# Strassen's seven block products for the output projections of both feed forwards

## The chip, the cores and the metric

One core of a Trainium2 chip runs the whole program. The metric is the device time of one execution in microseconds (us). Matmuls run on TensorE (PE), which writes to PSUM, a memory of 8 banks of 128 partitions x 512 fp32 here. VectorE (DVE), ScalarE (ACT) and GpSimd (POOL) do the elementwise work; DMAs are issued by SyncE (SP). The engines run their own queues in order and wait for each other by semaphores.

## The reference, cut to what matters

256 tokens of width 1024 pass through two transformer blocks. The last part of each block is a feed forward, and these two are what the change touches:

```python
def _swiglu(u, w_in, w_out):                       # first block, D_FF = 2816
    a = u @ w_in
    return (jax.nn.silu(a[..., :D_FF]) * a[..., D_FF:]) @ w_out

# second block, D_FF_2 = 4096
u = jnp.square(jax.nn.relu(jnp.einsum('bsd,df->bsf', h, w_mlp_in[l])))
x = x + gate_f * jnp.einsum('bsf,fd->bsd', u, w_mlp_out[l])
```

All values are fp32. In the first block the result is added to x without a gate.

## The kernel before

**Precision.** Every large matmul is made of three fp32r matmuls: an operand is split into a high part (a cast, `h` or `wh`) and a low part (the rest, `l` or `wl`), and `mm3` adds high x high, low x high and high x low into PSUM. `cols` loads weights by DMA into `raw` (128 x 1024), casts them on ACT to `wh` and subtracts on DVE to `wl`. So every 128 x 1024 piece of weights costs one DMA, one ACT step and one DVE step.

**A feed forward.** `ffn` walks over groups of hidden columns: 11 groups of 2 k-tiles (a k-tile is 128 hidden columns) in the first block, 8 groups of 4 in the second. The up projection (`dense_T`) makes the hidden values transposed: for a pair of k-tiles it takes 8 pieces of u, 2 columns of tiles and 3 matmuls each, 48 matmuls of 128x256 into one PSUM bank (twice that in the first block, which has two halves, the one through silu and the other one). Then come the elementwise steps: silu and a product in the first block (`glu`), relu and square in the second (`relu2`), and the split into `hT` high and low. The output projection (`out_steps`) takes one k-tile at a time: the hidden values of a k-tile are the stationary operand, 128 x 1024 of w_out the moving one, for both halves of the tokens. PSUM holds the 256 x 1024 result in 5 banks through the whole feed forward: two of 512 columns for the first 128 tokens, and 512, 256 and 256 for the second (`CUTS`). So a k-tile is 5 triples, 9 matmuls of 128x512 and 6 of 128x256. The last `lag` k-tiles finish the first half of the tokens ahead of the second, so that `resume` can start on it.

**What sets the order.** The code records operations, and a planner (`Plan.schedule`) puts them in order for each engine once, when the program is built, from its own costs and a table (`TUNING`, one row for each 140 of PE's large matmuls). `tt` records a tensor_tensor in two forms, and the planner takes DVE or POOL, whichever ends first by its costs. Buffers come from pools of slots: 37 of 4 KB a partition (`k4`), 14 of 2 KB, 12 of 1 KB, 8 PSUM banks. All operations are issued from one line, so the profile has a single line number, and groups are told apart by the tiles' names.

**The modulation** of the second block is computed in parts beside other work (`next_part`): four steps of 128x1024 on DVE a part (`raw<-raw,mod_c`). Six parts lie in the first feed forward and two in the second.

Of the kernel before, what the change touches and what calls it, by code (L numbers as in the profile page):

```python
# [40 lines left out]
def _constants():  # L41
# [63 lines left out]
FFN = [2] * 11  # L105
MLP = [4] * 8
# [167 lines left out]
class Plan:  # L274
# [362 lines left out]
class Net:  # L637
# [1012 lines left out]
    def swiglu(self, u, done):  # L1650
        nc, flow = self.nc, self.flow
        mods = []

        def swi(t, ac):
            sl = self.k(1, [P, S], nm="silu")
            nc.scalar.activation(sl, ac[:, :S], AF.Silu)
            yield
            nc.vector.tensor_tensor(sl, ac[:, S:], sl, ALU.mult)
            yield
            return sl  # L1660

        def glu(hT, aa, bb, n):
            sl = self.k(2, [P, n, S], nm="silu")
            nc.scalar.activation(sl, aa, AF.Silu)
            yield
            nc.vector.tensor_tensor(sl, bb, sl, ALU.mult)
            yield
            self.split(hT[0][0], hT[1][0], sl)
            yield

        def up(k0, n):
            hT = self.hidden(n)
            if k0 == 0:
# [11 lines left out]
        self.ffn("ffn", FFN, "w_ffn_out", up, done, LAG1, between)  # L1685


    def modulation(self):
# [78 lines left out]
    def block2_mix(self, x, u, done):  # L1767
# [263 lines left out]

        self.out_steps(self.out_accs(), [(act(k // 4), k, k) for k in range(KT)], "w_out_2", True, done, LAG2)

    def mlp(self, u, done):
        nc, flow = self.nc, self.flow

        def sq(t, ac):
            r, r2 = (self.k(2, [P, 512], nm="relu") for _ in range(2))
            nc.scalar.activation(r, ac, AF.Relu)
            yield  # L2040
            nc.vector.tensor_tensor(r2, r, r, ALU.mult)
            yield
            return r2

        def relu2(hT, i, ac):
            r, r2 = (self.k(2, [P, 2, S], nm="relu") for _ in range(2))
            nc.scalar.activation(r, ac, AF.Relu)
            yield
            nc.vector.tensor_tensor(r2, r, r, ALU.mult)
            yield  # L2050
            self.split(hT[0][0][:, 2 * i:2 * i + 2, :], hT[1][0][:, 2 * i:2 * i + 2, :], r2)
            yield

        def up(k0, n):
            hT = self.hidden(n)
            if k0 == 0:
                return hT, self.first_up(hT, u, n, [("w_mlp_in_2", 0)], sq)
            accs = self.dense_T(u, self.cols("w_mlp_in_2", k0 * P, (k0 + n) * P), n * P)
            return hT, [flow.start(relu2(hT, i, ac), "relu2") for i, ac in enumerate(accs)]

        def between(i):
            if 1 <= i <= 2:
                self.next_part()
            if i == 5:
                self.gate = self.mod(5)

        self.ffn("mlp", MLP, "w_mlp_out_2", up, done, 3, between)


LAG1, LAG2 = 6, 6  # L2070
MODF = (0, 2, 4, 5, 6, 7)
MODG = ((4, 0), (4, 1), (1, 0), (5, 0))

# [1 line left out]
def build(tc, a, out):  # L2075
    with ExitStack() as ctx:
        e = ctx.enter_context
# [7 lines left out]
        nc.lead = 0.0  # L2085
        n.setup()
        u, mem = n.mixer(x)
        u = n.memory_attention(x, u, mem)
# [78 lines left out]
```

## Time and profile before

| | us |
|---|---|
| median of 3 runs (762.37 to 763.64) | 762.38 |
| the profiled execution | 762.54 |
| its span | 760.7 |
| PE, DVE, ACT, POOL busy | 744.8, 571.7, 395.3, 42.0 |

The span runs from the first to the last instruction; the profiled execution's time has 1.8 us around it. Busy time of PE counts matmuls whose ends are modelled, and consecutive ones overlap, so the time of a matmul in a row is read from the start of one to the start of the next.

### The profile page before, as it was taken

To read this page: it belongs to the slowest core of one execution; us is meant where nothing else is said; L and a number is where in the kernel's file an instruction comes from. 1 tells how busy PE (TensorE), PEld (TensorE's weight loads), DVE (VectorE), ACT (ScalarE), POOL (GpSimd) and SP (SyncE) were. 2 spreads that over 40 slices of the span, in tenths; PEclk is the share of its full clock that TensorE was granted. 3 is DMA by queue.
4 is the path that set the end of the run, shared out by engine and by line. 5 is a ranking of instruction groups with operands and counts; after the bars stand their busy time and mean duration, and the time that the engine had idled before them with its cause. 6 is when DMAs were issued, how large, how long until landed. Compare 5 with 4: busy or idle time off the path is not lost.

```text
span 760.7 us, 13194 instructions
## 1 busy us (share of the span) xinstructions
PE 744.8 (98%) x5195; PEld 679.8 (89%) x5195; DVE 571.7 (75%) x936; ACT 395.3 (52%) x652; POOL 42.0 (6%) x50
## 2 busy tenths in 40 slices
PE   7999999999998999999999899999999999999998
PEld 5978899999897999999999788898887999999996
DVE  6999989799699995877453888887579976555512
ACT  6784774456387553443353646745347545454410
POOL 0012000000000000000000223021000000000000
PEclk9999999999999999999999999999999999999999
DMA  8828567965474887988868484555447777555401
GB/s 307 296 84 255 155 231 247 397 262 204 169 260 154 264 290 263 310 295 291 289 228 205 148 154 143 163 138 194 138 139 243 277 274 258 196 192 193 141 1 56
DMA packets 87763, 161.70 MB, mean 213 GB/s; under 512 B 8011, under 2 KB 44011, under 8 KB 87700
## 3 DMA queue, kind: packets, MB, share of 16 engines
q1 hardware_dynamic: 87700, 160.85, 64.6%
q8 instruction: 41, 0.67, 0.4%
q14 instruction: 22, 0.18, 0.1%
HBM read 159.75 MB, written 1.08 MB: 211 GB/s over the span
## 4 chain that ended last, share of the span: by engine, by line
PE 77%; DVE 11%; issue 6%; ACT 2%; DMA 2%; POOL 1%; SPq 0%; POOLq 0%; DVEq 0%; ACTq 0%
PE ps L634 77%; DVE wl L634 3%; DMA raw<-in_w_in_dram 2%; DVE s L634 1%; DVE sc L634 1%; DVE x L634 1%; DVE xn L634 1%; ACT wh L634 1%; DVE rp L634 1%; SPq L634 0%; POOL s L634 0%; DVE mk L634 0%; ACT prob L634 0%; DVE gt L634 0%; DVE aT L634 0%
## 5 line engine op out<-in xcount | busy, mean ns | idle before, releaser
L634 DVE TENSOR_TENSOR wl<-raw,wh 128x1024 fp32r<-128x1024 f32 (+4 forms) x237 | 279.1, 1203 | 66.0 <-ACT wh L634 49.5
L634 ACT ACTIVATE wh<-raw 128x1024 fp32r<-128x1024 f32 (+4 forms) x237 | 242.6, 1041 | 132.9 <-PE ps L634 30.3
L634 PE MATMUL ps<-aT,wh 128*128 128x256 f32 x1664 | 306.4, 284 | 0.0
L634 PEld LDWEIGHTS ps<-aT,wh 128*128 128x128 f32 x1664 | 257.9, 189 | 0.4 <-ACT wh L634 0.2
L634 PE MATMUL ps<-aT,wl 128*128 128x256 f32 x832 | 236.0, 284 | 0.0
L634 PE MATMUL ps<-wh,aT 128*128 128x512 f32 (+5 forms) x672 | 181.8, 357 | 2.1 <-ACT wh L634 1.3
L634 PEld LDWEIGHTS ps<-aT,wl 128*128 128x128 f32 x832 | 157.2, 189 | 0.5 <-issue 0.4
L634 PE MATMUL ps<-wh,hT 128*128 128x512 f32 (+1 forms) x540 | 140.1, 348 | 0.0
L634 PEld LDWEIGHTS ps<-wh,aT 128*128 128x128 f32 x672 | 118.6, 190 | 19.1 <-ACT wh L634 1.9
L634 PE MATMUL ps<-wl,aT 128*128 128x512 f32 (+5 forms) x336 | 117.3, 354 | 0.0
L634 PEld LDWEIGHTS ps<-wh,hT 128*128 128x128 f32 x540 | 93.9, 188 | 14.2
L634 PE MATMUL ps<-wl,hT 128*128 128x512 f32 (+1 forms) x270 | 94.1, 349 | 0.0
L634 PEld LDWEIGHTS ps<-wl,aT 128*128 128x128 f32 x336 | 63.5, 189 | 7.5
L634 DVE SCALAR_TENSOR_TENSOR raw<-raw,mod_c 128x1024 f32<-128x1024 f32 x48 | 57.3, 1218 | 6.8 <-DMA raw<-in_w_ada_dram 6.8
L634 PEld LDWEIGHTS ps<-wl,hT 128*128 128x128 f32 x270 | 50.7, 188 | 7.0
L634 POOL TENSOR_TENSOR s<-s,mhalf 128x1 f32<-128x1 f32 (+3 forms) x22 | 23.3, 1063 | 294.9 <-DVE s L634 284.2
L634 ACT ACTIVATE junk<-x 128x512 f32<-128x512 f32 (+1 forms) x29 | 16.1, 554 | 38.6 <-DVE x L634 36.5
L634 DVE TENSOR_TENSOR relu<-relu 128x512 f32<-128x512 f32 x16 | 10.9, 691 | 22.4 <-ACT relu L634 22.2
L634 ACT ACTIVATE prob<-ps,s 128x256 f32<-128x256 f32 (+1 forms) x48 | 20.0, 447 | 9.4 <-DVE s L634 9.4
L634 ACT ACTIVATE relu<-ps 128x512 f32<-128x512 f32 x16 | 9.5, 598 | 28.9 <-PE ps L634 28.3
L634 PE MATMUL ps<-ident,xn 128*128 128x128 f32 x96 | 19.4, 313 | 3.4 <-DVE xn L634 2.0
L634 ACT ACTIVATE hT<-silu 128x512 fp32r<-128x512 f32 x10 | 6.3, 632 | 31.0 <-DVE silu L634 31.0
(280 smaller groups left out, 647.1 us busy)
## 6 DMA issues: line engine op xcount, KB each, us to landing
raw<-in_w_in_dram SPq DMA_DIRECT2D x62, 512.0 KB, 6.3
raw<-in_w_ada_dram SPq DMA_DIRECT2D x48, 512.0 KB, 5.7
raw<-in_w_ffn_in_dram SPq DMA_DIRECT2D x44, 512.0 KB, 5.8
raw<-in_w_mlp_in_dram SPq DMA_DIRECT2D x32, 512.0 KB, 4.1
raw<-in_w_mlp_out_dram SPq DMA_DIRECT2D x32, 512.0 KB, 4.2
raw<-in_w_ffn_out_dram SPq DMA_DIRECT2D x22, 512.0 KB, 5.3
raw<-in_w_out_dram SPq DMA_DIRECT2D x16, 512.0 KB, 5.0
raw<-in_w_up_dram SPq DMA_DIRECT2D x6, 512.0 KB, 5.5
```

What stands on the lines that cost most here:

```text
L634: getattr(get[o.eng], name)(*map(real, args), **{k: real(v) for k, v in kw.items()})
```

## The change

For pairs of k-tiles the output projection becomes a product of 2 x 2 blocks. The hidden values are four blocks (two halves of the tokens, two k-tiles), the weights four (two k-tiles, left and right 512 columns), and the result four (two halves of the tokens, left and right columns). Strassen's scheme (in Winograd's form) needs seven block products in place of eight, from sums of blocks on both sides.

- `pair_sums` makes four more blocks of 128x128 from the four hidden blocks, then casts all that are needed (ACT) and takes the low parts (DVE: 128x384 and 128x512), in tiles `blocks`, `blockh`, `blockl`.
- `pair_weights` loads two rows of w_out as before and makes four sums of 128x512 (`sums<-raw,raw`, `raw<-raw`, `sums<-raw,raw`, `sums<-sums,raw`), each from two tensors in SBUF and by `tt`, so on DVE or POOL. Then it splits three pieces of 128x1024 and one of 128x512, where two of 128x1024 were split before.
- `pair_product` is 7 x 3 matmuls of 128x512. Each of the seven products has a PSUM bank of its own, in which all pairs add up; one bank is left for the up projections.
- `pair_end` forms the four result blocks from the seven banks and adds them to x, once for a feed forward.
- 9 of 11 pairs of the first feed forward and 14 of 16 of the second go this way; the last 2 pairs of each (`TAILF`, `TAIL`) go through `out_steps` as before, when the seven banks are free again.
- The order in the code is up projection p, then products of pair p - 2; in the first feed forward the first four products stand between the two up projections of a pair and three behind them.
- The planner's cost of a plain fp32 matmul has a floor of 0.213 in place of 0.109, one row of its table moves, and LAG1 is 4 in place of 6.

```diff
-            one = max(0.109, n / 600) if dt == F32 else max(0.054, n / 2250)
+            one = max(0.213, n / 600) if dt == F32 else max(0.054, n / 2250)
...
+    def pair_sums(self, a):
+        s = [a[:, i, :] for i in range(8)]
+        self.tt(s[4], s[0], s[2], ALU.add)
+        self.tt(s[5], s[1], s[0], ALU.subtract)
+        self.tt(s[6], s[4], s[1], ALU.subtract)
+        yield
+        self.tt(s[7], s[3], s[6], ALU.subtract)
+        yield
+        h, l = (self.k(4, [P, 8, P], F32R, nm=f"block{c}") for c in "hl")
+        for c in (slice(1, 4), slice(4, 8)):
+            self.nc.scalar.activation(h[:, c, :], a[:, c, :], AF.Copy)
+            self.nc.vector.tensor_tensor(l[:, c, :], a[:, c, :], h[:, c, :].bitcast(F32), ALU.subtract)
...
+    def pair_weights(self, w, k):
+        nc = self.nc
+        w0, w1 = (self.k(4, [P, DM], nm="raw") for _ in range(2))
+        for i, e in enumerate((w0, w1)):
+            nc.sync.dma_start(e, self.a[w][(k + i) * P:(k + i + 1) * P, :])
+        w2, w3 = self.k(4, [P, DM], nm="sums"), self.k(2, [P, 512], nm="sums")
+        lo, hi = slice(0, 512), slice(512, DM)
+        self.tt(w2[:, hi], w1[:, hi], w0[:, hi], ALU.subtract)
+        self.tt(w0[:, hi], w0[:, hi], w0[:, lo], ALU.subtract)
+        self.tt(w2[:, lo], w1[:, hi], w0[:, hi], ALU.subtract)
+        self.tt(w3, w2[:, lo], w1[:, lo], ALU.subtract)
+        out = []
+        for kb, e in ((4, w1), (4, w0), (4, w2), (2, w3)):
+            h, l = (self.k(kb, e.shape, F32R, nm=nm) for nm in ("wh", "wl"))
+            nc.scalar.activation(h, e, AF.Copy)
+            self.tt(l, e, h.bitcast(F32), ALU.subtract)
+            out.append((h, l))
...
+    BLOCKS = ((0, 1), (1, 3), (5, 6), (6, 5), (3, 2), (4, 4), (2, 7))
+    def pair_product(self, ps, blocks, w, first, last, which=slice(0, 7)):
+        for p, b in self.BLOCKS[which]:
+            self.mm3(ps[p], blocks[b], w[p], first, last)
...
+        for p in range(2, n):
+            self.main("mlp")
+            up(p)
+            if p - 2 < tail:
+                down(p - 2)
...
-LAG1, LAG2 = 6, 6
+LAG1, LAG2 = 4, 6
+TAIL, TAILF, LATE = 2, 2, 2
```

PE in the second feed forward. Before, the first 12 of a k-tile's 15 matmuls in the output projection (`ps` are the result's banks, `hT` the hidden values, `wh` and `wl` the weights):

```order
L634 MATMUL ps_7012<-wh_7380,hT_7496 128x512
L634 MATMUL ps_7012<-wh_7380,hT_7501 128x512
L634 MATMUL ps_7012<-wl_7393,hT_7496 128x512
L634 MATMUL ps_7020<-wh_7380,hT_7496 128x512
L634 MATMUL ps_7020<-wh_7380,hT_7501 128x512
L634 MATMUL ps_7020<-wl_7393,hT_7496 128x512
L634 MATMUL ps_7028<-wh_7380,hT_7496 128x512
L634 MATMUL ps_7028<-wh_7380,hT_7501 128x512
L634 MATMUL ps_7028<-wl_7393,hT_7496 128x512
L634 MATMUL ps_7035<-wh_7380,hT_7496 128x256
L634 MATMUL ps_7035<-wh_7380,hT_7501 128x256
L634 MATMUL ps_7035<-wl_7393,hT_7496 128x256
```

and now the first three of the seven products of a pair, behind the last matmul of an up projection:

```order
L634 MATMUL ps_8040<-aT_6866,wl_7938 128x256
L634 MATMUL ps_7106<-wh_7960,blockh_7894 128x512
L634 MATMUL ps_7106<-wh_7960,blockl_7902 128x512
L634 MATMUL ps_7106<-wl_7983,blockh_7894 128x512
L634 MATMUL ps_7114<-wh_7908,blockh_7894 128x512
L634 MATMUL ps_7114<-wh_7908,blockl_7902 128x512
L634 MATMUL ps_7114<-wl_7966,blockh_7894 128x512
L634 MATMUL ps_7121<-wh_7976,blockh_7894 128x512
L634 MATMUL ps_7121<-wh_7976,blockl_7902 128x512
L634 MATMUL ps_7121<-wl_7995,blockh_7894 128x512
```

A pair of k-tiles took 18 matmuls of 128x512 and 12 of 128x256; it now takes 21 of 128x512.

DVE in the second feed forward. Before, the steps for two pairs of k-tiles (four splits of the up projection's weights, four of the output's, in turns; square and split of the hidden values):

```order
L634 TENSOR_TENSOR wl_7517<-raw_7440,wh_7506 128x1024
L634 TENSOR_TENSOR wl_7540<-raw_7466,wh_7533 128x1024
L634 TENSOR_TENSOR wl_7561<-raw_7519,wh_7554 128x1024
L634 TENSOR_TENSOR wl_7590<-raw_7542,wh_7575 128x1024
L634 TENSOR_TENSOR wl_7608<-raw_7563,wh_7596 128x1024
L634 TENSOR_TENSOR wl_7629<-raw_7578,wh_7618 128x1024
L634 TENSOR_TENSOR wl_7657<-raw_7610,wh_7646 128x1024
L634 TENSOR_TENSOR wl_7684<-raw_7631,wh_7673 128x1024
L634 TENSOR_TENSOR relu_7707<-relu_7700 128x512
L634 TENSOR_TENSOR relu_7714<-relu_7709 128x512
L634 TENSOR_TENSOR hT_7721<-relu_7707,hT_7716 128x512
L634 TENSOR_TENSOR hT_7721<-relu_7714,hT_7716 128x512
```

and now the steps for one pair:

```order
L634 TENSOR_TENSOR wl_8044<-raw_7912,wh_7988 128x1024
L634 TENSOR_TENSOR wl_8058<-raw_7940,wh_8006 128x1024
L634 TENSOR_TENSOR sums_8046<-raw_7971,raw_7952 128x512
L634 TENSOR_TENSOR wl_8086<-raw_7971,wh_8029 128x1024
L634 TENSOR_TENSOR wl_8103<-raw_7952,wh_8080 128x1024
L634 TENSOR_TENSOR wl_8116<-sums_8046,wh_8096 128x1024
L634 TENSOR_TENSOR blocks_8129<-relu_8119 128x512
L634 TENSOR_TENSOR blocks_8129<-blocks_8129 128x128 x4
L634 TENSOR_TENSOR blockl_8144<-blocks_8129,blockh_8136 128x384
L634 TENSOR_TENSOR blockl_8144<-blocks_8129,blockh_8136 128x512
L634 TENSOR_TENSOR wl_8158<-sums_8089,wh_8123 128x512
```

A pair's steps on DVE went from six (four of 128x1024, two of 128x512) to 14.

POOL in the second feed forward, where it had no step before; now, for three pairs:

```order
L634 TENSOR_TENSOR sums_8046<-raw_7971,raw_7952 128x512
L634 TENSOR_TENSOR raw_7952<-raw_7952 128x512
L634 TENSOR_TENSOR sums_8089<-sums_8046,raw_7971 128x512
L634 TENSOR_TENSOR sums_8166<-raw_8091,raw_8074 128x512
L634 TENSOR_TENSOR raw_8074<-raw_8074 128x512
L634 TENSOR_TENSOR sums_8209<-sums_8166,raw_8091 128x512
L634 TENSOR_TENSOR blocks_8248<-blocks_8248 128x128
L634 TENSOR_TENSOR sums_8285<-raw_8211,raw_8196 128x512
L634 TENSOR_TENSOR raw_8196<-raw_8196 128x512
L634 TENSOR_TENSOR sums_8326<-sums_8285,raw_8211 128x512
```

Three of a pair's four sums of weights stand in POOL's queue, one in DVE's; DVE's one needs the first two of POOL's, and POOL's third needs DVE's.

## Rows read from the trace of the kernel before

**Rows 1.** The page: span, busy time by engine, the chain's shares.
```profile
span 760.7 us, 13194 instructions
PE 744.8 (98%) x5195; PEld 679.8 (89%) x5195; DVE 571.7 (75%) x936; ACT 395.3 (52%) x652; POOL 42.0 (6%) x50
...
PE 77%; DVE 11%; issue 6%; ACT 2%; DMA 2%; POOL 1%; SPq 0%; POOLq 0%; DVEq 0%; ACTq 0%
```

**Rows 2.** The chain in order of time: start, us, engine, tile, steps.
```profile
243.21 181.51 PE ps L634 x1345
...
575.68 179.29 PE ps L634 x1195
```

**Rows 3.** Busy time by stretch: stretch, length, then busy us and steps by engine.
```profile
core 0: us, PE busy (x) PEld busy (x) DVE busy (x) ACT busy (x) POOL busy (x), PEclk, DMA share, GB/s
242.00:428.60 186.60, 186.33 (x1388) 177.40 (x1388) 130.27 (x162) 83.74 (x105) 2.96 (x3) 1.00 0.79 253
...
576.00:757.00 181.00, 181.00 (x1213) 166.02 (x1211) 109.63 (x125) 77.94 (x93) 0.00 (x0) 1.00 0.54 182
```

**Rows 4.** Timeline of PE, one k-tile of an output product: start, us, step.
```profile
644.57 0.62 PE L634 MATMUL ps<-wh,hT 128*128 128x512 f32 x2
...
645.26 0.62 PE L634 MATMUL ps<-wh,hT 128*128 128x512 f32 x2
...
646.63 0.40 PE L634 MATMUL ps<-wh,hT 128*128 128x256 f32 x2
...
646.98 0.40 PE L634 MATMUL ps<-wh,hT 128*128 128x256 f32 x2
...
647.33 0.63 PE L634 MATMUL ps<-wh,hT 128*128 128x512 f32 x2
```

**Rows 5.** Timelines of DVE and POOL at 467.
```profile
466.94 3.49 DVE L634 TENSOR_TENSOR wl<-raw,wh 128x1024 fp32r<-128x1024 f32 x3
...
467.03 4.00 POOL L634 TENSOR_TENSOR rnat<-rp,rp 128x256 f32<-128x256 f32 x1 [4.46 <-DVE sp L634]
```

**Rows 6.** Timelines: 128x512 steps of DVE, and one of POOL.
```profile
753.51 1.28 DVE L634 TENSOR_TENSOR x<-x,gt 128x512 f32<-128x512 f32 x2
...
427.05 1.29 POOL L634 TENSOR_TENSOR xn<-x,modrow 128x512 f32<-128x512 f32 x1 [1.87 <-DVE x L634]
...
427.22 1.67 DVE L634 SCALAR_TENSOR_TENSOR xn<-xn,s,modrow 128x512 f32<-128x512 f32 x1
...
571.69 0.74 DVE L634 SCALAR_TENSOR_TENSOR xn<-xn,s,modrow 128x512 f32<-128x512 f32 x1
```

**Rows 7.** Groups by shape: busy us, mean ns, idle before; stretches 242:428, 600:740, 62:66.6.
```profile
L634 DVE SCALAR_TENSOR_TENSOR raw<-raw,mod_c 128x1024 f32<-128x1024 f32 x24 | 28.7, 1218 | 1.6 <-DMA raw<-in_w_ada_dram 1.6
...
L634 DVE TENSOR_TENSOR hT<-relu,hT 128x512 fp32r<-128x512 f32 x14 | 9.5, 692 | 0.3
L634 ACT ACTIVATE wh<-raw 128x1024 fp32r<-128x1024 f32 x46 | 47.9, 1056 | 46.5 <-DMA raw<-in_w_mlp_out_dram 21.1 <-DMA raw<-in_w_mlp_in_dram 16.1 <-PE ps L634 9.3
L634 ACT ACTIVATE relu<-ps 128x512 f32<-128x512 f32 x13 | 7.7, 597 | 25.7 <-PE ps L634 25.0
...
L634 DVE TENSOR_TENSOR wl<-raw,wh 128x536 fp32r<-128x536 f32 x1 | 1.3, 1260 | 0.0
```

**Rows 8.** Timeline of POOL, three places in the first 65 us.
```profile
23.48 0.46 POOL L634 TENSOR_TENSOR idxk<-rp,rp 128x128 f32<-128x128 f32 x1 [13.27 <-DVE rp L634]
...
49.23 2.83 POOL L634 TENSOR_TENSOR sp<-sp,ca 128x256 f32<-128x256 f32 x4 [20.40 <-DVE sp L634]
...
62.35 1.33 POOL L634 TENSOR_TENSOR qbn<-rp,rp 128x256 f32<-128x256 f32 x1 [3.20 <-DVE rp L634]
```

**Rows 9.** Timeline of DVE: the splits at the start of each feed forward.
```profile
243.74 1.21 DVE L634 TENSOR_TENSOR wl<-raw,wh 128x1024 fp32r<-128x1024 f32 x1
...
578.32 4.62 DVE L634 TENSOR_TENSOR wl<-raw,wh 128x1024 fp32r<-128x1024 f32 x4
```

**Rows 10.** Timeline of PE: the last output matmuls of each feed forward.
```profile
428.67 0.29 PE L634 MATMUL ps<-wl,hT 128*128 128x256 f32 x1
...
756.80 0.28 PE L634 MATMUL ps<-wl,hT 128*128 128x256 f32 x1
```

**Rows 11.** PE by stretch: length, busy us and steps, granted clock, DMA share, GB/s.
```profile
430.00:432.00 2.00, 1.24 (x3) 1.00 0.69 243
432.00:434.00 2.00, 0.97 (x4) 0.91 0.88 325
434.00:436.00 2.00, 2.00 (x9) 0.50 0.93 317
436.00:438.00 2.00, 2.00 (x8) 0.74 0.60 215
```

More of the change, by code (lines that the diff above doesn't have):

```diff
@@ new lines, in swiglu, with first, sums @@
+        tail = n - TAILF
+        blocks, pages, chains = {}, {}, {}
+        hT, ps = self.act_pair(), [self.acc() for _ in range(7)]
+        def first(t, ac):
+            o = yield from swi(t, ac)
+            pt, = yield from self.bank()
+            for j in range(2):
+                self.tr(pt[:, j * P:(j + 1) * P], o[:, j * P:(j + 1) * P])
+            self.pair_place(pages[0], pt[:, :S], t)
+            yield
+        def sums(p, *before):
+            yield from flow.after({0: list(before)})
+            blocks[p] = yield from self.pair_sums(pages[p])
@@ new lines, in silu, with glu @@
+        def silu(p, sl, ac):
+            nc.scalar.activation(sl, ac, AF.Silu)
+            yield
+        def glu(p, sl, ac):
+            yield from flow.after({0: chains["a", p]})
+            if p >= tail:
+                nc.vector.tensor_tensor(sl, ac, sl, ALU.mult)
+                yield
+                c, k = divmod(2 * (p - tail), 4)
+                self.split(*(e[c][:, k:k + 2, :] for e in hT), sl)
+                yield
+                return
+            pages[p] = self.pair_page()
+            flat = "p a b -> p (a b)"
+            nc.vector.tensor_tensor(pages[p][:, 0:4, :].rearrange(flat), ac.rearrange(flat), sl.rearrange(flat), ALU.mult)
+            yield
+            yield from sums(p)
@@ L1679, in between, with up, down @@
+        def up(p, part, fn, sl):
+            c0 = part * D_FF + p * S
+            ac, = self.dense_T(u, self.cols(w_in, c0, c0 + S), S)
+            chains["ab"[part], p] = flow.start(fn(p, sl, ac), "glu")
+        def down(p, which, w):
+            flow.need(chains["b", p])
+            self.pair_product(ps, blocks[p], w, p == 0, p == tail - 1, which)
         def between(i):
@@ L2034, in mlp, with squared @@
+    BLOCKS = ((0, 1), (1, 3), (5, 6), (6, 5), (3, 2), (4, 4), (2, 7))
+    def pair_product(self, ps, blocks, w, first, last, which=slice(0, 7)):
+        for p, b in self.BLOCKS[which]:
+            self.mm3(ps[p], blocks[b], w[p], first, last)
     def mlp(self, u, done):
         nc, flow = self.nc, self.flow
-        def sq(t, ac):
-            r, r2 = (self.k(2, [P, 512], nm="relu") for _ in range(2))
+        x, w_in, w_out = self.x, "w_mlp_in_2", "w_mlp_out_2"
+        n = 2 * sum(MLP) // 4
+        tail = n - TAIL
+        blocks, pages, hT = {}, {}, self.hidden(4)
+        def squared(ac, out):
+            r = self.k(2, [P, 512], nm="relu")
@@ L2039, in sq @@
             nc.scalar.activation(r, ac, AF.Relu)
             yield
[L2041 removed]
+            nc.vector.tensor_tensor(out, r, r, ALU.mult)
             yield
[L2043 to L2047, printed above, removed]
[L2048 to L2052 removed]
@@ L2054, in up, with first @@
[L2054 to L2062, printed above, removed]
+        def first(t, ac):
+            o = self.k(2, [P, 512], nm="relu")
+            yield from squared(ac, o)
+            pt, = yield from self.bank()
+            for j in range(4):
+                self.tr(pt[:, j * P:(j + 1) * P], o[:, j * P:(j + 1) * P])
+            for p in range(2):
+                self.pair_place(pages[p], pt[:, p * S:(p + 1) * S], t)
+            yield
@@ new lines, in sums, with pair, plain @@
+        def sums(p, *before):
+            yield from flow.after({0: list(before)})
+            blocks[p] = yield from self.pair_sums(pages[p])
+        def pair(p, ac):
+            pages[p] = self.pair_page()
+            yield from squared(ac, pages[p][:, 0:4, :].rearrange("p a b -> p (a b)"))
+            yield from sums(p)
+        def plain(p, ac):
+            o = self.k(2, [P, 2, S], nm="relu")
+            yield from squared(ac, o)
+            at = slice(2 * (p - tail), 2 * (p - tail) + 2)
+            self.split(hT[0][0][:, at, :], hT[1][0][:, at, :], o)
+            yield
@@ new lines, in mlp, with up, down @@
+        chains = {}
+        def up(p):
+            ac, = self.dense_T(u, self.cols(w_in, 2 * p * P, (2 * p + 2) * P), 2 * P)
+            chains[p] = flow.start((pair if p < tail else plain)(p, ac), "relu2")
+        ps = [self.acc() for _ in range(7)]
+        def down(p):
+            w = self.pair_weights(w_out, 2 * p)
+            flow.need(chains[p])
+            self.pair_product(ps, blocks.pop(p), w, p == 0, p == tail - 1)
+        self.main("mlp")
+        pages.update({p: self.pair_page() for p in range(2)})
@@ new lines, in mlp @@
+        wf = self.held(w_in, 0, 4 * P)
+        firsts = []
+        for t in range(NT):
+            flow.need(self.norms[t])
+            ac = self.acc()
+            self.dense_t(u, t, wf, ac)
+            firsts.append(flow.start(first(t, ac), f"first_{t}"))
+        for p in range(2):
+            chains[p] = flow.start(sums(p, *firsts), "relu2")
+        for p in range(2, n):
+            self.main("mlp")
+            up(p)
+            if p - 2 < tail:
+                down(p - 2)
+            if p in (4, 6):
@@ new lines, in pair_end, with add @@
+    def pair_end(self, ps, x, g=None):
+        nc = self.nc
+        tt = nc.vector.tensor_tensor
+        k = lambda: self.k(2, [P, 512], nm="sum")
+        p1, p2, p3, p4, p5, p6, p7 = ps
+        lo, hi = slice(0, 512), slice(512, DM)
+        def add(c, t, s):
+            if g is not None:
+                self.tt(c, c, g[:, s], ALU.mult)
+            self.tt(x[:, t, s], x[:, t, s], c, ALU.add)
+        c1, u = k(), k()
+        nc.scalar.activation(u, p1, AF.Copy)
+        tt(c1, p2, u, ALU.add)
+        tt(u, p6, u, ALU.add)
+        yield
+        u3 = k()
+        tt(u3, p7, u, ALU.add)
+        c4, c3 = k(), k()
+        nc.scalar.activation(c4, p5, AF.Copy)
+        tt(u, p5, u, ALU.add)
+        yield
+        tt(c3, u3, p4, ALU.subtract)
+        self.tt(c4, c4, u3, ALU.add)
+        tt(u, p3, u, ALU.add)
+        yield
+        add(c3, 0, lo)
+        add(c4, 0, hi)
+        add(c1, 1, lo)
+        add(u, 1, hi)
+        yield
```

66 lines of the change are left out of this document (50 added, 16 removed).

## Prediction

> **What bounds the kernel now.** I read the page first: TensorE (PE) is busy 98% of the span, VectorE (DVE) 75%, and the chain of waits lies on PE for 77% [rows 1]. The chain in order of time then says where PE alone sets the end: two stretches of some 180 us, which are the two feed forwards [rows 2]. The windows give these stretches a size: 186.6 us for the first, in which PE is never idle and DVE is busy 130 us, and 181.0 us for the second, with DVE busy 110 us [rows 3]. So what PE loses there is time won, as long as DVE, which feeds it, does not become the slower one: it has 56 and 71 us to spare. GpSimd (POOL) does 3.0 us of work in the first and none in the second. The profiled execution took 762.54 us (span 760.7); the median of the runs shown is 762.38. My sum is made against 762.54, and 0.2 us between the two decides nothing.
>
> **What PE saves.** A triple of 128x512 matmuls takes 0.69 us from start to start (644.57 to 645.26), a triple of 128x256 0.35 (646.63 to 646.98) [rows 4]. A k-tile of an output product has 3 triples of the first kind and 2 of the second: 2.77 us; from 644.57 to 647.33 it is 2.76. Two k-tiles cost 5.53 us. Seven block products cost 7 x 0.69 = 4.83. The gain is 0.70 us a pair. There are 9 pairs in the first feed forward and 14 in the second, so 23 x 0.70 = 16.1 us. The up projections keep their matmuls. If nothing else held PE, the time would be 762.5 - 16.1 = 746.4.
>
> **What DVE and POOL are given.** Steps of DVE in a row: three of 128x1024 take 3.49 us [rows 5], that is 1.14 apart; two of 128x512 take 1.28 [rows 6], 0.60 apart. By the line through these two, 128x384 takes 0.47 and 128x128 0.20. A step of the modulation with its accumulator read takes 28.7/24 = 1.20 [rows 7].
>
> Second feed forward, counted in the order of the changed kernel, from the first split of its weights to the last split that a block product needs. DVE: 70 of 128x1024 (79.8), 8 of the modulation (9.6), 49 of 128x512 (29.4), 14 of 128x384 (6.6), 40 of 128x128 (8.0), together 133 us. POOL: 49 of 128x512 and 16 of 128x128. A steady pair is 9.3 us of DVE (five 1024, four 512, one 384, three or four 128) beside 5.7 + 4.8 = 10.5 us of PE (16 triples of 0.35 for the up projection, then the products). DVE alone would just keep up. ScalarE has five casts of 1.06 us, a relu of 0.60 and two casts of blocks, some 7 us, and is no bound [rows 7].
>
> The question is whether POOL's steps run beside DVE's. Nearly all of both read two tensors in SBUF, and the trace has such meetings. POOL starts a 128x256 addition at 467.03, just behind the start of three weight splits on DVE, and ends at 471.03, 0.6 us after the last of them: 4.00 us instead of 0.71 [rows 5, 8]. At 427.22 DVE starts a 128x512 step while POOL is in one that takes 1.29; DVE's takes 1.67, where the same form takes 0.74 at 571.69 [rows 6]. And a 128x536 split takes 1.26 us where the 512-wide ones take 0.69, beside a POOL step begun at 62.35 [rows 7, 8]. Against that, four POOL steps at 49.23 ran at 0.71 each [rows 8] while DVE mostly read PSUM or a single tensor. I read it so: two such steps exclude each other, and the times add up.
>
> **The price of a POOL step.** Between the ends lies what it costs DVE: 0.93 us (1.67 - 0.74) and its whole 1.29 for 128x512. I take 1.20: in the first meeting POOL was already 0.17 us into its step when DVE started, which makes 1.10, and a handover from POOL to DVE or back will not be free. For 128x128, between nothing and the 0.46 of a step at 23.48 [rows 8]; I take 0.38. The second feed forward then has 49 x 1.20 + 16 x 0.38 = 64.9 us of POOL to put between 133 us of DVE: 198 us. A steady pair is 9.3 + 3 x 1.20 = 12.9 us and a little for blocks, against 10.5 of PE.
>
> The Trainium skill (SBUF — State Buffer, section Who interferes with whom) says that a VectorE instruction with two SBUF inputs and a GpSimd instruction that reads SBUF exclude each other, and that whoever comes first keeps the shared port for the whole instruction. By that rule the price is the whole 1.29 and 0.46, and the sum below would be 6 us higher for the second feed forward and 3 for the first. The trace agrees on the exclusion, but its one blocked DVE step lost 0.93.
>
> **The sum.** Before, DVE takes up this work at 578.32 [rows 9]. Nothing ahead of the feed forward is made shorter, so 578.3 + 198 = 776.5 is when the last split is there. PE then still has three of the seven products (2.1; the step that the last split feeds is fifth in the order) and four ordinary k-tiles (11.1): 789.7. From PE's last matmul to the end of the span it was 760.7 - 756.8 = 3.9 [rows 10]: 793.6, **33 us later** than now. The sums at the end (15 steps of DVE, 9 us) are hidden by the 11.1 us of the four k-tiles; without that cover some 4 us of them would show.
>
> First feed forward, counted the same way. DVE: 63 of 128x1024 (71.8), 24 of the modulation (28.8), 36 of 128x512 (21.6), 9 of 128x384 (4.2), 27 of 128x128 (5.4), two of 256 (0.7): 132 us. POOL: 26 of 128x512 (31.2), two of 128x1024 (2.4 each, twice a 512), 9 of 128x128 (3.4): 39 us. DVE starts at 243.74 [rows 9], so the last split is there at 415; behind it PE has half of an up projection (8 triples, 2.8), three products (2.1) and four k-tiles (11.1): 431. The matmuls of the present one end at 429.0 [rows 10]. That is +2. DVE's queue also has the product of the two up projections, which frees the one PSUM bank: it waits for the last 8 triples of PE (2.8 us) behind the last weight split, with one step of 1.2 us between. That is up to 1.6 us idle in each of 9 pairs, 0 to 14; POOL can use part of it, and I take 5. So **+7 us**.
>
> The remaining edits (a planner's cost for plain fp32 matmuls, one window of its table moved, the lag at the end) reorder steps in stages where PE is not short of work; I put them at 0, +-2. DMA carries the same weights. 762.5 + 33 + 7 = **802.5 us**.
>
> **The rivals.**
> (a) *POOL runs beside DVE.* Then a pair is bound by PE and the time is 746, or 750 with some waits at the ends. It decides at the point where DVE and POOL together fit into PE's pair: (10.5 - 9.3) / 3 = 0.4 us for a 128x512 step of POOL. For it speaks that the four steps at 49.23 were not hindered; against it the three meetings, each with more than 0.4 lost [rows 5 to 8]. Chance 0.13.
> (b) *The exclusion holds, but costs the low end:* 49 x 0.93 and nothing for the small ones is 46 us, 19 less than in the sum; the first feed forward then is bound by PE about as now. 802.5 - 19 - 7 = 776. It needs handovers without loss and no wait of DVE for PE. Chance 0.15.
> (c) *The single PSUM bank adds to the forecast:* DVE, late with its queue, frees the bank late, PE's next up projection waits, and DVE then waits for that. The full 14 us in the first feed forward and 1 us a pair in the second: 802.5 + 9 + 14 = 825. PE's clock can add to it: at 430 to 434 PE was busy 2.2 of 4 us, and the granted clock then stood at 0.50 (1.2 of 2.4 GHz) for two us and at a mean of 0.74 for two more [rows 11]. In a steady pair PE would be idle 2.4 us, so such a fall costs only where it is longer than the spare time. Chance 0.08.
> (d) That the change does not do what it says I leave out: the order shows 483 matmuls on blocks, 23 x 21.
>
> **How the numbers follow.** The forecast, DVE and POOL taking turns, has 0.64; its own range is 787 (price 0.93, no idle bank waits in the first feed forward) to 818 (price 1.29, 14 us of bank waits). For 8 in 10 I add (b) and most of (c): 770 to 825, with (a) and the far end of (c) left out. A measurement of this kernel tells 0.2% (1.5 us) from no change. Faster is (a): 0.13. Within 0.2% is a corner between (a) and (b): 0.02. Slower is the rest: 0.85.
>
> **What would show it.** Right: in the second feed forward DVE and POOL are busy nearly all the time, DVE's 128x512 and 128x1024 steps have means well above 0.69 and 1.22 us or POOL's stand far above 1.29, PE waits for DVE's wl in every pair and a pair lasts about 13 us; the first feed forward loses less than the second. The block products take 4.83 us a pair wherever PE does not wait. Wrong: PE still busy all through both stretches, with steps of DVE at 0.69 and 1.22 while POOL works; then (a). If PE's long waits are for the bank's release (silu or blocks) and not for wl, it is (c).

## The result, and the profile after

The changed kernel takes **829.88 us** (median; 828.0 to 831.79), 1.088 times the time of before (95% interval 1.0853 to 1.0908). The prediction was 802.5, with a range of 770 to 825: the direction was right, the size 27 us short, and the time lies 5 us outside the range. The profiled execution took 831.79 us, of which the span is 830.0.

The page of the changed kernel, the lines that answer to [rows 1]:

```profile
span 830.0 us, 13258 instructions
PE 759.3 (91%) x4988; PEld 681.6 (82%) x4988; DVE 740.2 (89%) x1112; ACT 443.0 (53%) x730; POOL 210.4 (25%) x152
...
DVE 22%; PE 16%; issue 4%; POOL 3%; ACT 2%; DMA 1%; POOLq 0%; SPq 0%; DVEq 0%; ACTq 0%
```

The chain of this profile is followed back only to 418 us, so its shares cover about half of the span; in that half DVE has more of it (22%) than PE (16%), where PE had 77% of the whole before, and POOL has 3%. DVE is busy 168 us longer and POOL 168. The busy time by stretch says where; the stretches are the first feed forward, the stage between, and the second (columns as in [rows 3]):

```profile
240.00:452.00 212.00, 193.17 (x1319) 179.35 (x1318) 191.20 (x235) 105.54 (x136) 62.60 (x42) 0.94 0.69 230
452.00:609.00 157.00, 148.81 (x845) 125.92 (x844) 128.61 (x219) 82.30 (x154) 26.76 (x19) 0.97 0.56 146
609.00:830.00 221.00, 185.88 (x1078) 164.71 (x1076) 211.01 (x224) 105.74 (x138) 105.63 (x63) 0.92 0.45 150
```

In the second feed forward DVE is busy 211 of 221 us and POOL 106, where it was 108 and nothing before. The granted clock of PE, 1.00 in both stretches of [rows 3], is now 0.94 and 0.92. The edges give the losses. The first feed forward's last output matmul starts at 451.91 and not 428.67 [rows 10]: +23.2. DVE's first split for the second feed forward starts at 608.90 and not 578.32 [rows 9]: +30.6, so the stage between gave 7.3. From there to the end it was 182.4 us and is 221.1: **+38.7**. (The expectations below say 22.6 and 8 for the first two; they took the edge a little earlier.)

What the second feed forward is made of stands in its groups of DVE and POOL by shape (busy us, mean ns):

```profile
L634 DVE TENSOR_TENSOR wl<-raw,wh 128x1024 fp32r<-128x1024 f32 x60 | 96.2, 1633 | 0.0
L634 DVE TENSOR_TENSOR wl<-sums,wh 128x1024 fp32r<-128x1024 f32 x14 | 24.1, 1724 | 0.0
L634 DVE TENSOR_TENSOR blockl<-blocks,blockh 128x512 fp32r<-128x512 f32 x14 | 18.1, 1296 | 1.1 <-ACT blockh L634 1.0
...
L634 POOL TENSOR_TENSOR sums<-sums,raw 128x512 f32<-128x512 f32 x14 | 30.6, 2189 | 48.4 <-DVE sums L634 48.2
L634 POOL TENSOR_TENSOR sums<-raw,raw 128x512 f32<-128x512 f32 x15 | 29.8, 1987 | 1.6 <-DVE wl L634 1.2 <-DMA raw<-in_w_mlp_in_dram 0.3
L634 POOL TENSOR_TENSOR raw<-raw 128x512 f32<-128x512 f32 x14 | 25.9, 1849 | 1.6 <-DVE sums L634 0.6
```

A split that took 1.22 us takes 1.63, and POOL's steps stand at 1.85 to 2.19, where one that was under way before DVE's next step took 1.26 (at 240.06). That is what the prediction asked for as a sign of turns being taken. The other sign, PE waiting for wl in each pair, is not there: PE's long waits name blocks in the first feed forward and relu in the second (us in total, times, longest). The last sections come back to that.

```profile
PE ps L634 <- DVE blocks L634: 12.7, 6, 4.7
...
PE ps L634 <- ACT relu L634: 22.6, 9, 6.1
```

### The profile page after: what moved, and what is told of

Same layout as the page of the kernel before. It is cut to its first block, busy times and chain, and to the rows that moved or that the text cites. A ratio compares the mean times of both kernels' runs of the same rounds, so it can differ in the third digit from the quotient of the medians.

```text
span 830.0 us, 13258 instructions
## 1 busy us (share of the span) xinstructions
PE 759.3 (91%) x4988; PEld 681.6 (82%) x4988; DVE 740.2 (89%) x1112; ACT 443.0 (53%) x730; POOL 210.4 (25%) x152
## 5 line engine op out<-in xcount | busy, mean ns | idle before, releaser
L634 PE MATMUL ps<-aT,wh 128*128 128x256 f32 x1664 | 327.5, 296 | 39.0 <-ACT relu L634 22.6
L634 DVE TENSOR_TENSOR wl<-raw,wh 128x1024 fp32r<-128x1024 f32 (+4 forms) x235 | 308.8, 1344 | 12.4 <-ACT wh L634 10.3
L634 ACT ACTIVATE wh<-raw 128x1024 fp32r<-128x1024 f32 (+4 forms) x237 | 242.0, 1037 | 102.7 <-POOL raw L634 28.7
L634 PE MATMUL ps<-wl,blockh 128*128 128x512 f32 x161 | 63.4, 394 | 1.0 <-DVE wl L634 1.0
L634 PE MATMUL ps<-wh,blockl 128*128 128x512 f32 x161 | 63.5, 394 | 0.0
L634 PE MATMUL ps<-wh,blockh 128*128 128x512 f32 x161 | 63.4, 394 | 0.0
L634 ACT ACTIVATE blockh<-blocks 128x384 fp32r<-128x384 f32 (+1 forms) x46 | 26.6, 578 | 68.7 <-DVE blocks L634 59.7
L634 POOL TENSOR_TENSOR sums<-sums,raw 128x512 f32<-128x512 f32 x21 | 46.3, 2204 | 54.0 <-DVE sums L634 53.8
L634 ACT ACTIVATE wh<-sums 128x1024 fp32r<-128x1024 f32 (+1 forms) x46 | 38.8, 842 | 34.3 <-DVE sums L634 18.7
L634 DVE TENSOR_TENSOR wl<-sums,wh 128x1024 fp32r<-128x1024 f32 (+1 forms) x31 | 49.3, 1599 | 0.0
L634 POOL TENSOR_TENSOR raw<-raw 128x512 f32<-128x512 f32 x21 | 39.4, 1878 | 20.2 <-DVE sums L634 19.2
L634 POOL TENSOR_TENSOR blocks<-blocks 128x128 f32<-128x128 f32 x25 | 17.7, 712 | 94.4 <-DVE blocks L634 60.7
L634 DVE TENSOR_TENSOR blockl<-blocks,blockh 128x384 fp32r<-128x384 f32 (+1 forms) x46 | 38.4, 836 | 2.2 <-ACT blockh L634 1.9
```

The source lines that it names most:

```text
L634: getattr(get[o.eng], name)(*map(real, args), **{k: real(v) for k, v in kw.items()})
```

## The experiments

### All pair steps on DVE, and each feed forward alone

```diff
 # dve_only: in pair_sums, pair_weights and pair_end
-        self.tt(w2[:, hi], w1[:, hi], w0[:, hi], ALU.subtract)
+        self.nc.vector.tensor_tensor(w2[:, hi], w1[:, hi], w0[:, hi], ALU.subtract)
...
 # mlp_only: swiglu as before; ff1_only: mlp as before
```

> The change with all sums and splits of the pairs on DVE, none on POOL. If DVE and POOL take turns (a POOL step of 128x512 costs about 1.20 us of DVE's time, the same step on DVE 0.60), the second feed forward gets 49 x 0.60 + 16 x 0.18 = 32 us shorter and the first up to 26 x 0.60 + 2 x 1.26 + 9 x 0.18 = 20: about 778 us, between 765 and 795. If POOL's steps run beside DVE's and the loss has another cause (the one PSUM bank), DVE has 75 x 0.60 + 25 x 0.20 = 50 us more to do and the time is 830 or more.

Measured **770.65 us** (ratio 1.0101, 1.0085 to 1.0117): 59 us less than the change, with 1213 steps on DVE in place of 1112. So POOL's help was the greater part of the loss; 8 us of it stay without that help. The same groups of DVE in the second feed forward, now alone in their stage:

```profile
L634 DVE TENSOR_TENSOR wl<-raw,wh 128x1024 fp32r<-128x1024 f32 x60 | 71.5, 1210 | 0.0
...
L634 DVE TENSOR_TENSOR wl<-sums,wh 128x1024 fp32r<-128x1024 f32 x14 | 16.9, 1210 | 0.0
...
L634 DVE TENSOR_TENSOR blockl<-blocks,blockh 128x512 fp32r<-128x512 f32 x14 | 9.5, 678 | 0.2
```

These three groups alone are 40.5 us shorter, with the same steps. And the two feed forwards by stretch:

```profile
243.00:424.00 181.00, 180.20 (x1302) 169.03 (x1300) 178.00 (x265) 104.54 (x135) 2.04 (x2) 1.00 0.83 269
576.00:749.00 173.00, 165.90 (x1030) 145.05 (x1028) 172.57 (x266) 104.27 (x138) 0.00 (x0) 0.99 0.54 186
```

In the first, PE is busy 180.2 of 181 us, and most of the 9 x 0.70 = 6.3 us that PE was to save are there: its last output matmul starts at 423.01 and not at 428.67 [rows 10], 5.7 us earlier. (DVE's last step that reads the output banks starts at 423.38, where it was 429.93, 6.6 earlier.) In the second DVE is busy 172.6 of 173 us and is the bound by itself: from its first split there (576.26) to the end (767.0) are 190.7 us, 8 more than the 182.4 of before.

> Block products in the second feed forward alone, the first as before. The trace of the changed kernel puts 38.7 us of the loss behind the start of the second feed forward's splits, 22.6 ahead of the end of the first and 8 between: about 803 us. By the prediction on record (33 and 7 us) 795.5. If the two stages disturb each other (the planner's order is made anew for the whole program), it is neither.

> Block products in the first feed forward alone, the second as before. By the trace of the changed kernel 762.4 + 22.6 + about 6 of the stage behind it = 791 us; by the prediction on record 769.5.

Measured **804.45** (1.0549, 1.0534 to 1.0565) and **787.69** (1.0328, 1.0311 to 1.0345). The two losses, 41.8 and 25.1 us, add up to 66.9 of the 67.5 of the change. So the stages hardly disturb each other, and the first feed forward's part is 23 to 25 us, more than three times what the prediction gave it.

### POOL steps that nothing waits for

```diff
 # pool_adds: dve_only, and in pair_weights of the second feed forward
+            more = self.k(2, [P, 512], nm="more")
+            for _ in range(3):
+                nc.gpsimd.tensor_tensor(more, w1[:, lo], w1[:, hi], ALU.add)
 # pool_memsets: eight of these instead
+                nc.gpsimd.memset(more, 0.0)
 # pool_copies: three of these instead
+                nc.gpsimd.tensor_copy(more, w1[:, hi])
```

> The kernel with all pair steps on DVE, and in each of the 14 pairs of the second feed forward three additions of 128x512 on POOL that nothing uses (both operands from the loaded weights in SBUF). DVE has no idle time in that stage. If a POOL step keeps DVE out, 42 x 1.07 us (the price read from the changed kernel's trace: 52.5 us of longer DVE steps for 49 POOL steps) = 45 us come on top of 770.6: 816, between 42 x 0.93 and 42 x 1.29 = 810 to 825. If POOL runs beside DVE, 771, at most 774.

> The same with eight memsets of 128x512 on POOL in each pair in place of the three additions: POOL is busy as long (112 x 0.48 = 54 us), but reads no tensor. If it is the reading of two tensors in SBUF that excludes, 771 to 774. If any POOL step, or the order and the semaphores around it, costs DVE time, 810 or more.

> The kernel with all pair steps on DVE, and in each pair of the second feed forward three copies of 128x512 on POOL from SBUF to SBUF, that nothing uses: one tensor read where the additions read two and the memsets none. If any read of SBUF by POOL keeps DVE out, 42 steps cost some 42 x 0.7 to 1.3 us: 800 to 825. If it takes two operands on POOL's side too, 769 to 774.

Measured **813.08** with additions (1.0664, 1.065 to 1.0679), **769.93** with memsets (1.0097, 1.0081 to 1.0112), **786.49** with copies (1.0318, 1.0303 to 1.0334). Against dve_only an addition costs 42.4 / 42 = 1.01 us, a copy 15.8 / 42 = 0.38, and 112 memsets nothing. The copies fit neither of their two forecasts (800 to 825, 769 to 774). No engine uses the results, and nearly all of the cost is the meeting itself: with the additions DVE is busy 37.9 us longer (740.8 for 702.9). In two places, 5.1 us together, DVE waits for a buffer that a POOL step still holds. The timeline of DVE in the kernel with additions shows it step by step; POOL's row is first:

```profile
654.76 28.23 POOL L634 TENSOR_TENSOR more<-raw 128x512 f32<-128x512 f32 x6 [3.36 <-DMA raw<-in_w_mlp_out_dram]
...
668.33 1.21 DVE L634 TENSOR_TENSOR wl<-raw,wh 128x1024 fp32r<-128x1024 f32 x1
669.46 0.67 DVE L634 TENSOR_TENSOR wl<-sums,wh 128x512 fp32r<-128x512 f32 x1
670.07 1.21 DVE L634 SCALAR_TENSOR_TENSOR raw<-raw,mod_c 128x1024 f32<-128x1024 f32 x1
671.21 0.07 DVE L634 DVE_READ_ACCUMULATOR raw<-raw,mod_c 128x1 f32 x1
671.21 2.30 DVE L634 SCALAR_TENSOR_TENSOR raw<-raw,mod_c 128x1024 f32<-128x1024 f32 x1
...
673.44 2.27 DVE L634 SCALAR_TENSOR_TENSOR raw<-raw,mod_c 128x1024 f32<-128x1024 f32 x1
...
675.64 2.27 DVE L634 SCALAR_TENSOR_TENSOR raw<-raw,mod_c 128x1024 f32<-128x1024 f32 x1
...
677.85 1.74 DVE L634 TENSOR_TENSOR sums<-raw,raw 128x512 f32<-128x512 f32 x1
679.51 1.22 DVE L634 SCALAR_TENSOR_TENSOR mod_s<-mod_s,mod_b 128x8 f32<-128x8 f32 x1
680.65 1.21 DVE L634 TENSOR_TENSOR wl<-raw,wh 128x1024 fp32r<-128x1024 f32 x1
681.78 1.76 DVE L634 TENSOR_TENSOR raw<-raw 128x512 f32<-128x512 f32 x1
...
729.13 1.73 DVE L634 TENSOR_TENSOR wl<-sums,wh 128x512 fp32r<-128x512 f32 x1 [3.86 <-POOL more L634]
```

POOL has six steps in 28.23 us, and six steps of DVE are longer by 1.06 to 1.09 us than the same forms elsewhere (2.30 for 1.21; 1.74 and 1.76 for 0.67; 1.22 for a step of 128x8 that took 0.15 in dve_only). One POOL step is one lengthened DVE step, whatever the DVE step's size.

The Trainium skill (SBUF — State Buffer, section Who interferes with whom) limits the exclusion to a GpSimd instruction that reads SBUF, which is how the memsets came to be the test. By that rule they cost nothing, and the trace agrees. By the same rule an addition or a copy should lock DVE out for its whole length. Here both fall 0.2 us short of it. While DVE stands still, an addition takes 1.26 us and a copy 0.62; where they meet a DVE step, they lengthen it by 1.06 to 1.09 and by 0.40. So the copy is cheaper because it is shorter. The rows of pool_copies, a copy alone and a DVE step that met one (1.62 for 1.21):

```profile
710.57 0.62 POOL L634 COPY more<-raw 128x512 f32<-128x512 f32 x1
...
629.31 1.62 DVE L634 SCALAR_TENSOR_TENSOR raw<-raw,mod_c 128x1024 f32<-128x1024 f32 x1
```

### Weight sums left out

```diff
-        self.tt(w2[:, hi], w1[:, hi], w0[:, hi], ALU.subtract)
...
-        self.tt(w3, w2[:, lo], w1[:, lo], ALU.subtract)
...
-        for kb, e in ((4, w1), (4, w0), (4, w2), (2, w3)):
+        for kb, e in ((4, w1), (4, w0), (4, w1), (2, w0[:, lo])):
```

> The four sums of weights of a pair are left out and the seven products use the pieces of w_out as they are, so the output projections of the pairs are not those of the reference; splits, block sums and matmuls stay. DVE then has about 8.8 us a pair beside 10.5 of PE and POOL next to nothing. If DVE and POOL were the bound, PE sets the pace again: about 750 us, 744 to 757. If the one PSUM bank costs by itself, even with DVE to spare, it stays at 765 or more.

Measured **768.31** (1.0081, 1.0058 to 1.0104). This one tells nothing apart: with the sums gone, the planner gave POOL splits in their place (16 of 128x512 at a mean of 2.39 us and four of 128x1024 at 3.25) beside 23 block sums of 128x128, so POOL still met DVE, and the experiment had not taken away what it was to take away. It should have kept the splits on DVE.

### The bank freed by ACT

```diff
 # act_frees_bank, in glu of the first feed forward
+            bc = self.k(2, [P, 2, S], nm="bcopy")
+            nc.scalar.activation(bc, ac, AF.Copy)
+            yield
-            nc.vector.tensor_tensor(pages[p][:, 0:4, :].rearrange(flat), ac.rearrange(flat), sl.rearrange(flat), ALU.mult)
+            nc.vector.tensor_tensor(pages[p][:, 0:4, :].rearrange(flat), bc.rearrange(flat), sl.rearrange(flat), ALU.mult)
```

> The change, with one thing moved in the first feed forward: ACT copies the second up projection's bank to SBUF as soon as PE is done, so that the bank no longer waits for the product step in DVE's queue. If the one bank, freed late by DVE, is what makes the first feed forward lose 22.6 us and not the 7 of the prediction, 8 to 15 us come back: 815 to 822. If DVE and POOL alone set its length, the bank only moves PE's idle time: within 4 us of 829.9, or a little more for ACT's added 0.6 us a pair.

Measured **832.09** (1.0923, 1.0897 to 1.0948). My theory of the moment, that the bank freed late by DVE's product step makes the first feed forward lose 15 us more than predicted, falls as it was put. PE's waits only moved. In the changed kernel PE waits 15.9 us in that stage for DVE's product step (12.7 named blocks, 3.2 silu). Now it waits 21.0 us for ACT's silu, which frees the bank of the first of a pair's two up projections. The longest of these waits is 8.53 us, and that silu stands in ACT's queue behind casts that wait for weights.

```profile
417.36 0.58 PE L634 MATMUL ps<-aT,wh 128*128 128x256 f32 x1 [8.53 <-ACT silu L634]
```

With all steps on DVE, the same single bank is freed by the same step of DVE, and PE waits for it nowhere in the two feed forwards. So the bank alone costs nothing: it is where a late queue shows on PE. No run had a second bank for the up projections, so what the one bank adds once a queue is late was not measured.

### The first feed forward: was there DVE time to spare?

```diff
 # pool_adds_first: as pool_adds, in the first feed forward (9 pairs)
-            w = self.pair_weights(w_out, 2 * q) if 0 <= q < tail else None
+            w = self.pair_weights(w_out, 2 * q, True) if 0 <= q < tail else None
```

> The kernel with all pair steps on DVE, and three unused additions of 128x512 on POOL in each of the 9 pairs of the first feed forward. There PE sets the pace: DVE has by the prediction's count 152 us to do beside 182 of PE. If a stage's length is the larger of the two sums, as the prediction took it, 27 x 1.01 us (the price measured in the second feed forward) bring DVE to 179 and cost nothing to 3 us: 770 to 774. If DVE's spare time can't be used, since it works no further ahead of PE than the one bank and the buffers let it, 10 us or more of the 27 come through: 780 to 798.

Measured **799.19** (1.0485, 1.0468 to 1.0501): 28.5 us more than dve_only for 27 additions, 1.06 us each, and 1 us above the higher of the two forecasts. The whole price comes through, in a stage where PE had looked like the bound. In dve_only both engines are full there up to 395.9 (PE 151.7 and DVE 149.8 of 152.2 us), and then PE has to wait for a split:

```profile
243.70:395.90 152.20, 151.70 (x1119) 143.59 (x1118) 149.77 (x223) 83.90 (x102) 0.00 (x0) 1.00 0.82 273
...
395.93 0.50 PE L634 MATMUL ps<-wl,blockh 128*128 128x512 f32 x1 [0.53 <-DVE wl L634]
```

From there the chain lies on PE for 21 us, and PE needs 27 us to its last output matmul (423.01). So the stage's length is not the larger of two sums, DVE's 152 us and PE's 182. It is DVE's steps up to the splits that PE waits for, plus what PE has left behind them, and each us added ahead of these splits comes through. The last split that a product needs ends at 402.82 in dve_only and at 431.52 with the additions, 28.7 us later. Whether the one bank and the buffers keep DVE from working further ahead, as the expectation supposed, was not tested. The same stretch with the additions:

```profile
243.00:424.00 181.00, 164.00 (x1139) 152.26 (x1139) 179.01 (x230) 84.62 (x105) 46.03 (x27) 0.95 0.70 234
```

DVE was full already and is now as busy (179.0 for 178.0); PE is 16 us short of its work.

### The planner's edits

```diff
 # the kernel before, with
+            one = max(0.213, n / 600) if dt == F32 else max(0.054, n / 2250)
+LAG1, LAG2 = 4, 6
```

> The kernel before, with only the floor of 0.213 in the planner's cost of a plain fp32 matmul and LAG1 at 4. The stage between the feed forwards grew by 4.5 to 8.2 us in every kernel with the change's edits, also where the first feed forward was the old one (5.0). If these two edits do it, 762.4 + 5 = 767.5, 765 to 769; if they cost nothing, as the prediction put it (0, +-2), 760.5 to 764.5.

Measured **764.9** (1.0033, 1.0021 to 1.0046): 2.45 us more, between its two forecasts. The prediction had 0, +-2. By the edges used above, the first feed forward ends 0.8 us earlier here (427.89), and the stage between is 3.2 us longer (to 580.73), of the 7.3 of the changed kernel. In dve_only, which has these edits and no pair step on POOL, it is 3.6 us longer (423.01 to 576.26). So about half of the 7.3 goes with the edits and half with POOL. Of POOL's half 2.0 us can be read: in the changed kernel POOL starts the first weight sums of the second feed forward at 603.64, into the norm's steps of DVE, and three of these (from 603.71) take 3.28 us, where they took 1.27 in dve_only. Where the other 1.7 us lie is open.

### A version that beats both

```diff
 # best_b: dve_only, and
-            nc.vector.tensor_tensor(out, r, r, ALU.mult)
+            nc.scalar.activation(out, r, AF.Square)
...
-            if p in (4, 6):
-                self.next_part()
...
-LAG1, LAG2 = 4, 6
-TAIL, TAILF, LATE = 2, 2, 2
-MODF = (0, 2, 4, 5, 6, 7)
+LAG1, LAG2 = 6, 6
+TAIL, TAILF, LATE = 2, 3, 2
+MODF = (0, 1, 2, 4, 5, 6, 7, 8)
...
 # best_b alone, best_a without it
-            one = max(0.213, n / 600) if dt == F32 else max(0.054, n / 2250)
+            one = max(0.109, n / 600) if dt == F32 else max(0.054, n / 2250)
```

> All pair steps on DVE; the square of the second feed forward on ACT (14 + 4 steps of 0.60 us less on DVE); its two parts of the modulation moved to the first feed forward (9.6 us less on DVE there); three pairs through the ordinary way at the end of the first feed forward and its lag back at 6. DVE then has some 10.6 us a pair beside PE's 10.5, so PE should set the pace nearly everywhere: 22 pairs x 0.70 = 15.4 us saved, less some 5 us for the stage between and the end: 749 to 757. If DVE or ACT still is the bound, 762 or more.

> The best kernel so far (756.1), with the floor in the planner's cost back at 0.109. If that edit is a part of what the stage between the feed forwards lost, 752 to 755; if not, 756.

Measured **756.07** (0.9915, 0.9902 to 0.9927) and **755.35** (0.9909, 0.9895 to 0.9922), so the second is 7 us faster than the kernel before; the 0.7 us between the two lies within their spread. The page of the second:

```profile
PE 732.8 (97%) x4997; PEld 662.7 (88%) x4997; DVE 688.7 (91%) x1186; ACT 447.8 (59%) x743; POOL 42.8 (6%) x51
...
PE 72%; DVE 18%; DMA 4%; ACT 2%; issue 2%; POOL 1%; SPq 1%; POOLq 0%; DVEq 0%; ACTq 0%
```

The chain is on PE again, and POOL is back near the 42 us of before. Seven block products do pay here, once POOL has no part in them and DVE has been relieved: of the 74.5 us between the change and best_b, 59 came from moving the pairs' steps to DVE and 15 from the other edits together. These edits were not tried one by one, nor in the kernel before.

## Why the prediction was right, and where it failed

**Right: the saving on PE.** The seven products of a pair take 4.88 us in the rows below (810.14 to 815.02), forecast 4.83. dve_only's first feed forward ends 5.7 us earlier than the one of before by PE's last output matmul; 9 x 0.70 is 6.3.

**Right: DVE and POOL take turns, and the price.** Taken was 1.20 us for a 128x512 step of POOL between ends of 0.93 and 1.29; measured were 1.01 (pool_adds) and 1.06 (pool_adds_first), so the ends hold and the value between them was 0.15 to 0.2 too high. Rival (a), POOL beside DVE, is excluded by pool_adds, and rival (b), the low end of 0.93, by these prices and the time. The Trainium skill's rule (SBUF — State Buffer, Who interferes with whom), a lock for the whole instruction, would have made the price 1.29; the exclusion is as that section says, the price 0.2 to 0.3 below it.

**Right in the sum, in part by luck: the second feed forward's 198 us.** From DVE's first split at 608.90 to the end of the last that a product needs it took 196.1. DVE was busy 189.5 of these and idle 6.6, which the forecast had at nothing. An estimate from the groups' means, here and in dve_only, puts 55 us of the busy time down to POOL, where the forecast had 64.9, and leaves 134 for DVE's own steps, forecast 133. So the price was 10 us too high, and the idle time made up for most of it. The views are DVE, ACT and PE at that place:

```profile
608.90 2.35 DVE L634 TENSOR_TENSOR wl<-raw,wh 128x1024 fp32r<-128x1024 f32 x2
...
803.23 1.81 DVE L634 TENSOR_TENSOR wl<-sums,wh 128x1024 fp32r<-128x1024 f32 x2
...
802.26 0.63 ACT L634 ACTIVATE wh<-sums 128x512 fp32r<-128x512 f32 x1 [0.23 <-POOL sums L634]
...
803.74 0.58 ACT L634 ACTIVATE relu<-ps 128x512 f32<-128x512 f32 x1
...
804.37 0.50 PE L634 MATMUL ps<-aT,wh 128*128 128x256 f32 x2 [2.02 <-ACT relu L634]
...
810.14 0.39 PE L634 MATMUL ps<-wh,blockh 128*128 128x512 f32 x1
...
815.02 0.39 PE L634 MATMUL ps<-wh,hT 128*128 128x512 f32 x1
...
826.03 0.28 PE L634 MATMUL ps<-wl,hT 128*128 128x256 f32 x1
```

**Failed, 8 us: "PE then still has three of the seven products (2.1) and four ordinary k-tiles (11.1)."** When the last split ends at 805.04, PE has only just begun the last up projection. It had waited for its bank, that is for a relu which stands in ACT's queue behind a cast that waits for POOL's sum. So PE still has 5.1 us of that, seven products (4.9) and the four k-tiles: 21.0 us from the last split to the start of the last matmul (826.03), not 13.2.

**Failed, 15 us: "behind it PE has half of an up projection (8 triples, 2.8), three products (2.1) and four k-tiles (11.1)".** This is the largest miss. The first feed forward's last split was foreseen at 415, plus 5 of waits, and ended at 421.32, which is right in the total. (DVE's first split came 2.9 us late, at 246.67 and not 243.74: POOL's first sums met the norm's steps ahead of it.) But:

```profile
417.88 3.44 DVE L634 TENSOR_TENSOR wl<-raw,wh 128x1024 fp32r<-128x1024 f32 x2
421.25 0.68 DVE L634 TENSOR_TENSOR silu<-ps,silu 128x512 f32<-128x512 f32 x1
...
421.98 0.79 PE L634 MATMUL ps<-aT,wh 128*128 128x256 f32 x2 [3.23 <-DVE silu L634]
...
430.30 0.39 PE L634 MATMUL ps<-wh,blockh 128*128 128x512 f32 x1
...
433.10 0.40 PE L634 MATMUL ps<-aT,wh 128*128 128x256 f32 x2
...
438.80 0.39 PE L634 MATMUL ps<-wh,blockh 128*128 128x512 f32 x1
...
440.88 0.39 PE L634 MATMUL ps<-wh,aT 128*128 128x512 f32 x1
...
451.91 0.28 PE L634 MATMUL ps<-wl,aT 128*128 128x256 f32 x1
```

Behind the last two splits DVE has the step that frees PE's bank. Only then, at 421.98, can PE start the next to last up projection; behind it come four products (430.30), the last up projection (433.10), three products (438.80) and the k-tiles (440.88 to 452.2). That is 30.9 us behind the last split and not 16. Of the excess 8.3 us are a whole up projection, 2.8 four products, 2.9 the other half of the last one, 0.7 a wait. The order of DVE's and PE's queues, which I had, shows all of it: I counted PE's work behind the last split by what needs that split, and not by what stands behind it in PE's own queue and was still waiting. In dve_only, where the step that frees the bank stands ahead of the last splits (DVE starts it at 395.79), the same tail is 20.2 us (402.82 to the start of the last output matmul at 423.01; here 30.6 to 451.91). pool_adds_first says the same of the whole stage: DVE had no time to spare ahead of its last splits, so each us that POOL took came through.

**The clock** is a part of it. The up projection at 421.98 takes 8.3 us where the next takes 5.7:

```profile
410.00:420.00 10.00, 8.53 (x60) 7.35 (x58) 9.43 (x9) 6.18 (x8) 2.35 (x1) 1.00 0.42 141
420.00:430.00 10.00, 8.02 (x46) 8.02 (x47) 6.30 (x7) 4.86 (x5) 0.00 (x0) 0.66 0.81 261
```

PE stood still from 418.76 to 421.98, and the granted clock of the ten us around it is a mean of 0.66, that is a part of the time at the lower level of 1.2 GHz. The two up projections differ by 2.6 us, and behind the last split nothing covers that.

**Failed, 7 us: "I put them at 0, +-2", the remaining edits.** The stage between lost 7.3 us. Of these 3.2 come with the edits in a kernel without block products (planner_edits, 2.45 us in all). The rest goes for the most part with POOL, whose first sums met the norm's steps of DVE; the forecast had priced such meetings only from the first split on.

The account: 802.5 + 16.2 (first feed forward: 23.2 for 7) + 7.3 + 5.7 (second: 38.7 for 33) = 831.7, the profiled execution's time within 0.1. **Rival (c)** had named waits for the bank and a falling clock, with 825 and a chance of 0.08. The sign asked for it was seen (PE waits for relu and blocks, not for wl), and the late bank is the link by which PE's tail behind the last split grew. But (c) put the cost into waits of DVE for PE, up to 1.6 us in each pair, and it came at the ends of the stages, so that its number lies nearest is luck. By dve_only the one bank costs nothing where no queue is late.

## What to carry to other kernels

Before work is moved from VectorE to GpSimd, add the two engines' times as if they were one, for steps that read two tensors in SBUF on VectorE and at least one on GpSimd: here a GpSimd addition cost VectorE 1.0 us to spare it 0.6. Where one engine becomes the bound, count a stage to its very end: all that the new bound has to do in it, and behind its last step everything that the other engines' own queues still hold, not only what depends on that step. A wait seen on PE for a buffer's release names the queue that is late, and moving the release to another queue helps only if that queue is not late as well.

## What the runs showed of the hardware that I had not expected

- A POOL addition of 128x512 that comes first takes 1.26 us, but costs DVE 1.01 to 1.09, also when the DVE step that meets it has only 128x8 elements (1.22 us for 0.15).
- POOL can be kept out for long. In pool_adds one addition is under way for 17.7 us from 654.76 and one for 35.2 from 691.20, while DVE runs one two-tensor step after another. In pool_adds and pool_copies together eight of POOL's steps take 13 us or more. Each of them gets its turn at the first break in DVE's row: four times at a read of the accumulator (at 671.21 in the rows above), twice at a step that reads PSUM, twice where DVE itself stands still because POOL holds a buffer (the 3.86 us above). Once in, POOL met DVE step after DVE step; why it then needs no further break the runs don't show.
- What POOL's step costs DVE goes with the step's length, if it reads SBUF: 1.06 to 1.09 us for an addition that takes 1.26 alone, 0.40 for a copy that takes 0.62, and nothing for a memset of 0.53, although the 112 memsets kept POOL busy some 59 us.
